# Moving a mixer's GpSimd arithmetic to VectorE, and keeping split weight operands in DRAM between two token halves

## The chip, the cores and the metric

The kernel runs on one core of a Trainium2 chip. The metric is the device time of one execution in microseconds (us). Five engines of the core work side by side, each on its own instruction stream: TensorE (PE in the profile; its weight loads are PEld), VectorE (DVE), ScalarE (ACT), GpSimd (POOL) and SyncE (SP), which here issues DMA transfers only. A measurement of this kernel tells apart differences of about 0.2%.

## The reference, cut to what matters

A two-layer decoder trunk over 1024 tokens of width 1024, in float32. Layer 0 mixes with a gated recurrence (HGRN2, four heads) and a retention (four heads); layer 1 mixes with an mLSTM (four heads). Each mixer and each MLP is wrapped in RMS norms.

```python
for l in range(DEPTH):
    g = norm_g[l]
    h = rmsnorm(x, g[0])
    y = even_mixer(h, ...) if l % 2 == 0 else odd_mixer(h, ...)
    x = x + rmsnorm(y, g[1])
    h = rmsnorm(x, g[2])
    x = x + rmsnorm(sq_relu_mlp(h, mlp_w1[l], mlp_w2[l]), g[3])
...
def even_mixer(h, w_in, ...):
    p = h @ w_in                       # 1024 x 5120
    hq, hf, hi, hgate, rq, rk, rv, rgate = jnp.split(p, splits, axis=-1)
    ...                                # scans over chunks, per-head norm, silu gates
    return y @ w_out
```

## The kernel before

**Stages.** The order is: even mixer on the first 512 tokens, even mixer on the second 512, first MLP on all tokens, odd mixer on the first half, odd mixer on the second, second MLP. Recurrent state goes from the first half to the second, so the halves are in order, and each half reads all weights of its mixer.

**Products.** A float32 product is made of three TensorE products of fp32r operands: every operand is split into `hi` (a rounded copy, made by ACT) and `lo` (the rest, a subtraction on DVE), and hi·hi, hi·lo and lo·hi are accumulated. On top of that a 2 x 2 block product is made of seven block products instead of eight (`combine`), which needs sums and differences of the weight blocks before they are split: four elementwise operations per set of four blocks, in `operands`. In the mixers a job is a *pair* (`p...`, `proj_pair`: seven operands of 128x512) or a *group* (`g...`, `proj_group`: seven operands of 128x1024, 24 matmuls of 256 columns for each). An even half has eight pairs and six groups, an odd half four and four, each followed by an output projection (`proj_tok`) whose 12 or 8 weight tiles are split without sums.

**The weight pipeline.** `raws` lists the weight tiles in the order of use; `pump` loads them on SP's queue into a ring of four buffers (`raw`, 512 KB each), and frees one when its last reader is done. `plan` lists the units; `next_units` has units prepared two ahead of the one it gives out. A unit is a pair of buffers `whi`, `wlo`, three of each. `split_w` (L157 to L161) makes hi on ACT and lo on DVE. The sums of `operands` (the helper is at L185 to L190) run on GpSimd in the mixers (`eng=nc.gpsimd`, rows of L190) and on DVE in the MLPs (L188). One buffer `ws` holds the sum of a21 and a22.

**Order.** The order within each engine's stream is made at build time by a scheduler that takes the ready instruction that stands first in the program. `tc.high_priority(offset=-100)` in `split_w`, in the MLP's `operands` and in `rest_operands` makes instructions count as if they stood 100 instructions later.

**Other GpSimd work.** In `right_sums` (L409) two of four differences of activation blocks, in `post_finish` (L496) the residual sum of the first half's output, in `silu_gate` (L609) the product of gate and sigmoid, in `rope` (L724) the last sum. The small [128 x 1] steps of the norms (`rsq`, L127 and L128) are on GpSimd too, and so are the DMA issues of the MLP's hidden activations (L1148).

**Chains.** Beside its products the even mixer has a chain for each HGRN head (`hg_chain`, L620): seven levels, each with four small score matmuls, a predicated copy (L664) and three products on DVE (L676 to L678) that the next level reads. Scans over four chunks follow (`hg_scan`, `rt_scan`, `ml_scan`).

Of the kernel before, what the change touches and what calls it, by code (L numbers as in the profile page):

```python
# [7 lines left out]
F32 = mybir.dt.float32  # L8
F32R = mybir.dt.float32r
# [6 lines left out]
P = 128  # L16
# [53 lines left out]
def hybrid_kernel(ctx, tc, x, norm_g, pv_d, cs_d, mk_d, dec_d, cos_d, sin_d, wg_d, gb_d, w_ev, w_od, w_mlp, out):  # L70
# [59 lines left out]

    raws = []
    MLP_UNITS = [0, 2, 4, *range(60), 60, 63, 61, 62, 60, 63, 61, 62]
    raws += [w_ev[u] for u in [*range(UE)] * 2]
    raws += [w_mlp[u] for u in MLP_UNITS]
    raws += [w_od[u] for u in [*range(UO)] * 2]
    raws += [w_mlp[64 + u] for u in MLP_UNITS]
    NRAW = 4
    loaded, count = [], {"taken": 0, "freed": 0, "given": 0}
# [1 line left out]
    def pump():  # L140
        while len(loaded) < min(count["freed"] + NRAW, len(raws)):
            i = len(loaded)
            raw = wp.tile([P, 1024], F32, tag="raw", bufs=NRAW, name=f"raw{i}")
            nc.sync.dma_start(out=raw, in_=raws[i])
            loaded.append(raw)

    def take_raw():
# [8 lines left out]

    def split_w(dst, src):  # L157
        hi, lo = dst
        with tc.high_priority(offset=-100):
            nc.scalar.copy(out=hi, in_=src)  # L160
            nc.vector.tensor_tensor(out=lo, in0=src, in1=hi.bitcast(F32), op=ALU.subtract)  # L161

    def new_pair(i):
        return (wp.tile([P, 1024], F32R, tag="hi", name=f"whi{i}"),
# [6 lines left out]
        free_raw()  # L171
        return hl

    def operands(wide, eng):

        if wide:
            a11, a21, a22, a12 = (take_raw() for _ in range(4))
            t = wp.tile([P, 1024], F32, tag="ws", bufs=1, name="ws")
        else:
            r1, r2 = take_raw(), take_raw()  # L180
            a11, a12 = r1[:, 0:512], r1[:, 512:1024]
            a21, a22 = r2[:, 0:512], r2[:, 512:1024]
            t = wp.tile([P, 1024], F32, tag="ws", bufs=1, name="ws")[:, 0:512]

        def op(o, x0, x1, f):  # L185
            if eng is nc.vector:
                with tc.high_priority(offset=-100):
                    eng.tensor_tensor(out=o, in0=x0, in1=x1, op=f)  # L188
            else:
                eng.tensor_tensor(out=o, in0=x0, in1=x1, op=f)  # L190

        op(t, a21, a22, ALU.add)
        yield a11
        yield t
        op(a21, a11, a21, ALU.subtract)
        op(a11, t, a11, ALU.subtract)
        yield a11
        yield a12
        op(a12, a12, a11, ALU.subtract)
        if wide:  # L200
            free_raw()
        yield a21
        if wide:
            free_raw()
        yield a12
        yield a22
        free_raw(2)

    def rest_operands():

        r1, r2 = take_raw(), take_raw()
        a11, a12 = r1[:, 0:512], r1[:, 512:1024]
        a21, a22 = r2[:, 0:512], r2[:, 512:1024]
        t = wp.tile([P, 1024], F32, tag="ws", bufs=1, name="ws")[:, 0:512]

        def op(o, x0, x1, f):
            with tc.high_priority(offset=-100):
                nc.vector.tensor_tensor(out=o, in0=x0, in1=x1, op=f)

        op(t, a21, a22, ALU.add)  # L220
        op(a21, a11, a21, ALU.subtract)
        op(a11, t, a11, ALU.subtract)
        yield a11
        yield t
        yield a21
        op(a12, a12, a11, ALU.subtract)
        yield a12
        yield a22
        free_raw(2)

    def pair_preps(n, eng=nc.gpsimd, begun=0):
        gen = {}
        todo = [(p, o, o == 0, o == last) for p in range(n) for last in [4 if p < begun else 6] for o in range(last + 1)]

        def prep(j):
            def run(i):
                hl = new_pair(i)
                for e, (p, o, first, last) in enumerate(todo[2 * j:2 * j + 2]):
                    if first:
                        gen[p] = rest_operands() if p < begun else operands(False, eng)  # L240
                    c = slice(e * 512, (e + 1) * 512)
                    split_w((hl[0][:, c], hl[1][:, c]), next(gen[p]))
                    if last:
                        next(gen[p], None)
                return hl
            return run
        return [prep(j) for j in range((len(todo) + 1) // 2)]

    def group_preps(eng=nc.gpsimd):
        gen = []  # L250

        def prep(o):
            def run(i):
                hl = new_pair(i)
                if o == 0:
                    gen.append(operands(True, eng))
                split_w(hl, next(gen[0]))
                if o == 6:
                    next(gen[0], None)
                return hl  # L260
            return run
        return [prep(o) for o in range(7)]

    BEGUN = 3

    def mlp_plan():
        units = [std_prep] * BEGUN + pair_preps(16, nc.vector, BEGUN)
        for _ in range(7):
            units += group_preps(nc.vector)
        return units + [std_prep] * 8  # L270

    plan = []
    for _ in range(2):
        for job in EV_JOBS:
            plan += group_preps() if job[0] == "g" else pair_preps(1)
        plan += [std_prep] * 12
    plan += mlp_plan()
    for _ in range(2):
        for job in OD_JOBS:
            plan += group_preps() if job[0] == "g" else pair_preps(1)  # L280
        plan += [std_prep] * 8
    plan += mlp_plan()
    ready = []

    def take_first():
# [3 lines left out]
    def next_units(j):  # L289
        n = count["given"]  # L290
        count["given"] += j
        while len(ready) < min(n + 3, len(plan)):
            ready.append(plan[len(ready)](len(ready)))
        return ready[n:n + j]
# [113 lines left out]

    def right_sums(stage):  # L409
        b11, b12, t1, t2, b21, t3, b22, t4 = (z[:, c] for z in stage for c in (L, R))  # L410
        for o, x0, x1, eng in ((t1, b12, b11, nc.vector), (t2, b22, t1, nc.vector),
                               (t3, b22, b12, nc.gpsimd), (t4, b21, t2, nc.gpsimd)):
            eng.tensor_tensor(out=o, in0=x0, in1=x1, op=ALU.subtract)  # L413

    def right_split(stage, k, p11, tiles):
        def split(dst, src):
# [76 lines left out]
        junk = sm.tile([P, 512], BF16, tag="junk", bufs=1, name="junk")  # L493
        nc.scalar.activation(out=junk, in_=y, func=AF.Square, accum_out=ss[t][:, n:n + 1])

    def post_finish(s, half, t, parts, ss, grow, tags=("z0", "z1"), eng=nc.gpsimd):  # L496
        tot = sm.tile([P, 1], F32, tag="tot", name=f"tot{s}_{half}_{t}")
        nc.gpsimd.tensor_tensor(out=tot, in0=ss[t][:, 0:1], in1=ss[t][:, 1:2], op=ALU.add)
        rs = sm.tile([P, 1], F32, tag="rs", name=f"rs{s}_{half}_{t}")
        rsq(rs, tot, 1.0 / D)  # L500
        xt = rg.tile([P, D], F32, tag=tags[t % len(tags)], name=f"xr{s}_{half}_{t}")
        nc.sync.dma_start(out=xt, in_=x_src(s, half * NT + t))
        s2 = sm.tile([P, 2], F32, tag="s2", name=f"s2{s}_{half}_{t}")
        for n in range(2):
            c = slice(n * 512, (n + 1) * 512)
            tmp = rg.tile([P, 512], F32, tag="tmp", bufs=2, name="ptmp")
            nc.vector.scalar_tensor_tensor(out=tmp, in0=parts[n], scalar=rs, in1=grow[:, c],
                                           op0=ALU.mult, op1=ALU.mult)
            eng.tensor_tensor(out=xt[:, c], in0=xt[:, c], in1=tmp, op=ALU.add)
            if s < 3:  # L510
                junk = sm.tile([P, 512], BF16, tag="junk", bufs=1, name="junk")
                nc.scalar.activation(out=junk, in_=xt[:, c], func=AF.Square, accum_out=s2[:, n:n + 1])
        nc.sync.dma_start(out=x_dst(s, half * NT + t), in_=xt)
        if s < 3:
            r = cp.tile([P, 1], F32, tag=f"rstd{half}_{t}", name=f"r{s}_{half}_{t}")
            nc.gpsimd.tensor_tensor(out=r, in0=s2[:, 0:1], in1=s2[:, 1:2], op=ALU.add)
            rsq(r, r, 1.0 / D)
            rstd[half, t] = r
        return xt
# [19 lines left out]
    def mixer_last(s, yT):  # L539
# [11 lines left out]
        xn = []  # L551
        for t in range(NT):
            post_sq(p1[t], t, 1, ss)
            xt = post_finish(s, 1, t, [y0[t], p1[t]], ss, grow, XT, nc.vector)
            parts = [kt.tile([P, HALF], F32, tag="kt", name=f"xk{s}_{t}_{n}") for n in range(2)]
            for n in range(2):
                nc.scalar.activation(out=parts[n], in_=xt[:, n * 512:(n + 1) * 512], func=AF.Copy, scale=rstd[1, t])
# [51 lines left out]
    def silu_gate(c, nm):  # L609
        for j in range(2):  # L610
            tmp = rg.tile([P, 2, 256], F32, tag="tmp", bufs=2, name=nm + f"sg{j}")
            nc.scalar.activation(out=tmp, in_=c[j], func=AF.Sigmoid)
            nc.gpsimd.tensor_tensor(out=c[j], in0=c[j], in1=tmp, op=ALU.mult)

    def scan_states(home, nm):

# [107 lines left out]
    def rope(c, cos, sin):  # L724
# [1 line left out]
        nc.vector.tensor_tensor(out=tmp[64:128], in0=c[0:64], in1=sin[0:64], op=ALU.mult)  # L726
        nc.vector.tensor_tensor(out=tmp[0:64], in0=c[64:128], in1=sin[64:128], op=ALU.mult)
        nc.vector.tensor_tensor(out=c, in0=c, in1=cos, op=ALU.mult)
        nc.gpsimd.tensor_tensor(out=c, in0=c, in1=tmp, op=ALU.add)

    def rt_keys(half, h, hT, cos, sin):
        nm = f"rt{half}_{h}"
# [691 lines left out]
```

## Time and profile before

| | |
|---|---|
| median of 3 runs | 2698.22 us (2695.55 to 2700.66) |
| the profiled execution | 2706.18 us, span 2704.4 us |
| busy: PE, PEld | 2467.0 us, 2239.8 us |
| busy: DVE, ACT, POOL | 1980.1 us, 1204.1 us, 780.4 us |
| moved by DMA | 335.91 MB, mean 124 GB/s |

Busy times are unions over the span; a matmul's end is modelled, so a busy PE may still be slower than it could be. The clock column (PEclk) is the share of full speed that the chip granted to TensorE.

### The profile page before, as it was taken

What the parts mean: (1) busy time and instruction counts of PE and PEld (TensorE: products, weight loads), DVE (VectorE), ACT (ScalarE), POOL (GpSimd) and SP (SyncE); (2) the same over time, 40 slices, a digit from 0 to 9 for tenths busy, and PEclk for the clock granted to TensorE, in tenths of its full rate; (3) what the DMA queues carried; (4) which work ended last, traced back from release to release, by engine and by line L of the source; (5) the groups of instructions that cost most, each with busy time, mean ns of one, the idle gap of its engine ahead of it and who ended that gap; (6) DMA issues with size and microseconds to landing.
All of it is one profiled execution on the core that took longest, in us unless ns stands there. A gap on an engine that the chain in (4) does not pass through costs nothing. (4 is left out here: it accounts for less than half of the span.)

```text
span 2704.4 us, 41553 instructions
## 1 busy us (share of the span) xinstructions
PE 2467.0 (91%) x16432; PEld 2239.8 (83%) x16432; DVE 1980.1 (73%) x2574; ACT 1204.1 (45%) x2080; POOL 780.4 (29%) x895
## 2 busy tenths in 40 slices
PE   6989998898897999999998688988988999999997
PEld 6888888898885888899997588888866888899996
DVE  7898868889748666657774798789757666766774
ACT  5444454444445443443344544554455434443332
POOL 5665437665311111100001345376320111100000
PEclk8999999999998999999999899999999999999999
DMA  3222323122232434453453222232233433554353
GB/s 137 69 73 78 110 86 118 63 79 71 94 140 102 168 144 156 171 198 126 160 172 125 103 87 79 100 133 69 96 134 108 169 145 140 210 178 136 129 174 140
DMA packets 92836, 335.91 MB, mean 124 GB/s; under 512 B 10848, under 2 KB 10976, under 8 KB 92640
## 3 DMA queue, kind: packets, MB, share of 16 engines
q1 hardware_dynamic: 75744, 272.42, 29.6%
q0 software_dynamic: 16896, 60.83, 5.9%
q8 instruction: 129, 2.11, 0.3%
q14 instruction: 67, 0.55, 0.1%
HBM read 255.61 MB, written 77.59 MB: 123 GB/s over the span
## 5 line engine op out<-in xcount | busy, mean ns | idle before, releaser
L160 ACT CAST whi<-raw 128x512 fp32r<-128x512 f32 (+1 forms) x590 | 469.6, 812 | 684.4 <-PE p_0x L1168 72.4
L161 DVE TENSOR_TENSOR wlo<-raw,whi 128x512 fp32r<-128x512 f32 (+1 forms) x590 | 583.7, 1005 | 192.3 <-ACT whi L160 174.1
L1279 POOL TENSOR_TENSOR rs<-pm 128x1 f32<-128x1 f32 (+1 forms) x7 | 2.2, 321 | 635.2 <-ACT junk L1263 635.2
L190 POOL TENSOR_TENSOR raw<-raw,raw 128x1024 f32<-128x1024 f32 (+1 forms) x64 | 151.1, 2361 | 83.3 <-DVE wlo L161 41.5
L160 ACT CAST whi<-ws 128x512 fp32r<-128x512 f32 (+1 forms) x90 | 70.4, 782 | 101.4 <-POOL ws L190 34.7
L190 POOL TENSOR_TENSOR raw<-ws,raw 128x512 f32<-128x512 f32 (+1 forms) x44 | 88.6, 2014 | 62.1 <-DVE wlo L161 42.1
L161 DVE TENSOR_TENSOR wlo<-ws,whi 128x512 fp32r<-128x512 f32 (+1 forms) x90 | 96.8, 1075 | 9.0 <-ACT whi L160 9.0
L190 POOL TENSOR_TENSOR ws<-raw,raw 128x1024 f32<-128x1024 f32 x20 | 51.1, 2555 | 39.3 <-DMA raw<-in_w_ev_dram 30.8
L322 DVE TENSOR_TENSOR ya<-p_0x,ya 128x1024 f32<-128x1024 f32 x26 | 31.8, 1222 | 34.9 <-PE p_0x L1169 34.9
L188 DVE TENSOR_TENSOR raw<-raw,raw 128x1024 f32<-128x1024 f32 (+1 forms) x54 | 52.0, 963 | 0.5
L413 POOL TENSOR_TENSOR xb_a<-xb_a,xb_a 128x256 f32<-128x256 f32 x32 | 34.2, 1079 | 56.4 <-ACT xb_a L479 50.4
L190 POOL TENSOR_TENSOR ws<-raw 128x512 f32<-128x512 f32 x24 | 36.3, 1513 | 46.8 <-DMA raw<-in_w_od_dram 25.5
L190 POOL TENSOR_TENSOR raw<-raw 128x512 f32<-128x512 f32 x24 | 36.7, 1528 | 32.4 <-DVE wlo L161 32.4
L1166 PE MATMUL p_0v<-whi,h_5R1h 128*128 128x256 f32 x128 | 36.6, 286 | 3.1 <-ACT h_5R1h L1019 3.1
L1166 PE MATMUL p_0v<-whi,h_1R0h 128*128 128x256 f32 x128 | 35.9, 281 | 2.9 <-ACT m_15h L340 2.9
L1168 PE MATMUL p_0v<-whi,h_5R1l 128*128 128x256 f32 x128 | 36.7, 287 | 1.8 <-DVE h_5R1l L1020 1.8
L1166 PE MATMUL p_0x<-whi,h_4L1h 128*128 128x256 f32 x128 | 35.8, 280 | 1.1 <-ACT whi L160 1.1
L1166 PE MATMUL p_0x<-whi,h_2L0h 128*128 128x256 f32 x128 | 36.0, 281 | 0.6 <-ACT ya L1173 0.6
L1169 PE MATMUL p_0v<-wlo,h_5R1h 128*128 128x256 f32 x128 | 36.4, 285 | 0.0
L1168 PE MATMUL p_0z<-whi,h_3L4l 128*128 128x256 f32 x128 | 35.9, 280 | 0.3 <-DVE h_3L4l L1020 0.3
L1168 PE MATMUL p_0v<-whi,h_1R0l 128*128 128x256 f32 x128 | 35.8, 280 | 0.0
L1169 PE MATMUL p_0x<-wlo,h_2L0h 128*128 128x256 f32 x128 | 35.8, 279 | 0.0
(5385 smaller groups left out, 10111.4 us busy)
## 6 DMA issues: line engine op xcount, KB each, us to landing
raw<-in_w_mlp_dram SPq DMA_DIRECT2D x142, 512.0 KB, 3.7
h<-hid SPq DMA_DIRECT2D x112, 512.0 KB, 4.3
raw<-in_w_ev_dram SPq DMA_DIRECT2D x104, 512.0 KB, 3.3
raw<-in_w_od_dram SPq DMA_DIRECT2D x64, 512.0 KB, 3.3
xs<-xr SPq DMA_DIRECT2D x24, 512.0 KB, 2.9
xr<-xs SPq DMA_DIRECT2D x24, 512.0 KB, 5.2
xn<-in_x_dram SPq DMA_DIRECT2D x8, 512.0 KB, 3.8
xr<-in_x_dram SPq DMA_DIRECT2D x8, 512.0 KB, 5.3
```

The costliest lines, as they stand in the source:

```text
L160: nc.scalar.copy(out=hi, in_=src)
L161: nc.vector.tensor_tensor(out=lo, in0=src, in1=hi.bitcast(F32), op=ALU.subtract)
L188: eng.tensor_tensor(out=o, in0=x0, in1=x1, op=f)
L190: eng.tensor_tensor(out=o, in0=x0, in1=x1, op=f)
L322: nc.vector.tensor_tensor(out=o, in0=x0, in1=x1, op=ALU.add)
L413: eng.tensor_tensor(out=o, in0=x0, in1=x1, op=ALU.subtract)
L1166: nc.tensor.matmul(a, h[:, c], hi[:, w], start=first and k == 0 and t % 2 == 0, stop=False, skip_group_check=True)
L1168: nc.tensor.matmul(a, l[:, c], hi[:, w], start=False, stop=False, skip_group_check=True)
L1169: nc.tensor.matmul(a, h[:, c], lo[:, w], start=False, stop=k == 3, skip_group_check=True)
L1279: nc.gpsimd.tensor_tensor(out=rs[:, z], in0=ss[half][:, 0, z], in1=ss[half][:, 1, z], op=ALU.add)
```

## The change

GpSimd's elementwise work of the mixers goes to DVE (sums of weight blocks, two differences in `right_sums`, the residual sum, the gate product, the last sum of `rope`). GpSimd keeps the [128 x 1] steps and the DMA issues of the hidden activations. In a mixer's first half each group's unit is also written to DRAM, hi and lo, right after its split. In the second half a group does no sums and no splits: units 0, 2 and 4 come through the ring of four raw buffers (two buffers for each, freed when the unit after next is asked for), units 1, 3, 5 and 6 are loaded into `whi` and `wlo`. Pairs and output projections are as before. All `high_priority(offset=-100)` are gone, in the MLPs too.

```diff
+    RING = (0, 2, 4)
+    kept = {}
+    def mixer_raws(w, jobs, n):
+        first, second, u = [], [], 0
+        for job in jobs:
+            m = 4 if job[0] == "g" else 2
+            mine = [w[u + i] for i in range(m)]
+            u += m
+            first += mine
+            if m == 4:
+                kept[n, job] = [[tc.dram_tile([P, 1024], F32, name=f"kw{n}_{job}_{o}{z}") for z in "hl"] for o in range(7)]
+                mine = [(F32R, z) for o in RING for z in kept[n, job][o]]
+            second += mine
+        last = [w[i] for i in range(u, n)]
+        return first + last + second + last
...
     def split_w(dst, src):
         hi, lo = dst
-        with tc.high_priority(offset=-100):
-            nc.scalar.copy(out=hi, in_=src)
-            nc.vector.tensor_tensor(out=lo, in0=src, in1=hi.bitcast(F32), op=ALU.subtract)
+        nc.scalar.copy(out=hi, in_=src)
+        nc.vector.tensor_tensor(out=lo, in0=src, in1=hi.bitcast(F32), op=ALU.subtract)
...
         def op(o, x0, x1, f):
-            if eng is nc.vector:
-                with tc.high_priority(offset=-100):
-                    eng.tensor_tensor(out=o, in0=x0, in1=x1, op=f)
-            else:
-                eng.tensor_tensor(out=o, in0=x0, in1=x1, op=f)
+            nc.vector.tensor_tensor(out=o, in0=x0, in1=x1, op=f)
...
-    def group_preps(eng=nc.gpsimd):
+    def group_preps(keep=None):
...
+                if keep:
+                    for d, z in zip(keep[o], hl):
+                        nc.sync.dma_start(out=d, in_=z.bitcast(F32))
                 return hl
...
+    held = {}
+    def kept_preps(keep):
+        def prep(o):
+            def run(i):
+                if o in RING:
+                    held[i] = 2
+                    return take_raw(), take_raw()
+                hl = new_pair(i)
+                for d, z in zip(keep[o], hl):
+                    nc.sync.dma_start(out=z.bitcast(F32), in_=d)
+                return hl
+            return run
+        return [prep(o) for o in range(7)]
+    def mixer_plan(jobs, n, outs):
+        units = []
+        for prep in (group_preps, kept_preps):
+            for job in jobs:
+                units += prep(kept[n, job]) if job[0] == "g" else pair_preps(1)
+            units += [std_prep] * outs
+        return units
...
     def next_units(j):
         n = count["given"]
         count["given"] += j
+        for i in [i for i in held if i < n]:
+            free_raw(held.pop(i))
...
-        for o, x0, x1, eng in ((t1, b12, b11, nc.vector), (t2, b22, t1, nc.vector),
-                               (t3, b22, b12, nc.gpsimd), (t4, b21, t2, nc.gpsimd)):
-            eng.tensor_tensor(out=o, in0=x0, in1=x1, op=ALU.subtract)
+        for o, x0, x1 in ((t1, b12, b11), (t2, b22, t1), (t3, b22, b12), (t4, b21, t2)):
+            nc.vector.tensor_tensor(out=o, in0=x0, in1=x1, op=ALU.subtract)
...
-            eng.tensor_tensor(out=xt[:, c], in0=xt[:, c], in1=tmp, op=ALU.add)
+            add(xt[:, c], xt[:, c], tmp)
...
-            nc.gpsimd.tensor_tensor(out=c[j], in0=c[j], in1=tmp, op=ALU.mult)
+            nc.vector.tensor_tensor(out=c[j], in0=c[j], in1=tmp, op=ALU.mult)
...
-        nc.gpsimd.tensor_tensor(out=c, in0=c, in1=tmp, op=ALU.add)
+        nc.vector.tensor_tensor(out=c, in0=c, in1=tmp, op=ALU.add)
```

## Rows read from the trace of the kernel before

**Rows 1.** The page's first part: the whole span, busy time of each engine.

```profile
span 2704.4 us, 41553 instructions
PE 2467.0 (91%) x16432; PEld 2239.8 (83%) x16432; DVE 1980.1 (73%) x2574; ACT 1204.1 (45%) x2080; POOL 780.4 (29%) x895
```

**Rows 2.** Busy time by stretch: even halves, MLP's two stages, odd halves.

```profile
core 0: us, PE busy (x) PEld busy (x) DVE busy (x) ACT busy (x) POOL busy (x), PEclk, DMA share, GB/s
28.00:335.00 307.00, 277.53 (x2196) 265.43 (x2197) 266.25 (x364) 136.10 (x265) 179.38 (x156) 0.95 0.25 83
...
424.00:730.00 306.00, 269.97 (x2147) 259.69 (x2146) 263.99 (x343) 136.21 (x266) 186.65 (x173) 0.96 0.25 83
...
842.00:1138.00 296.00, 293.41 (x1244) 235.62 (x1245) 198.44 (x305) 122.24 (x214) 41.20 (x60) 0.99 0.42 152
1138.00:1480.00 342.00, 324.97 (x2677) 320.80 (x2676) 230.27 (x208) 138.52 (x158) 10.25 (x12) 0.99 0.48 160
1480.00:1530.00 50.00, 28.01 (x194) 22.06 (x193) 36.70 (x49) 28.98 (x58) 20.97 (x18) 0.83 0.38 137
1530.00:1700.00 170.00, 151.24 (x1150) 145.88 (x1151) 148.54 (x223) 84.29 (x166) 76.86 (x86) 0.95 0.25 83
...
1767.00:1945.00 178.00, 154.86 (x1158) 148.73 (x1158) 154.86 (x223) 89.24 (x184) 105.30 (x110) 0.94 0.29 103
```

**Rows 3.** The same view, around single groups: two of the first half, one of the second.

```profile
80.50:111.30 30.80, 26.67 (x234) 25.49 (x234) 29.64 (x35) 12.24 (x20) 17.61 (x10) 1.00 0.20 69
287.50:320.80 33.30, 29.30 (x246) 28.28 (x246) 31.00 (x37) 12.52 (x21) 14.31 (x8) 0.95 0.30 103
471.30:505.20 33.90, 29.13 (x227) 28.65 (x226) 29.58 (x33) 13.43 (x26) 22.77 (x19) 0.90 0.19 63
```

**Rows 4.** PE's waits, 424:730 (who, released by: total us, times, longest), one row.

```profile
PE hg_1s L648 <- DVE hg_1ca L667: 4.3, 1, 4.3
```

**Rows 5.** By line and shape, 28:335, DVE, last ACT: count, busy us, mean ns, idle.

```profile
L161 DVE TENSOR_TENSOR wlo<-raw,whi 128x1024 fp32r<-128x1024 f32 x39 | 52.9, 1357 | 2.4 <-ACT whi L160 2.3
L677 DVE TENSOR_TENSOR hg_0qk<-hg_0qk,hg_0ts 128x256 f32<-128x256 f32 x7 | 8.4, 1195 | 0.0
L677 DVE TENSOR_TENSOR hg_3ca<-hg_3ca,hg_3ca 128x256 f32<-128x256 f32 x7 | 6.2, 886 | 0.0
L677 DVE TENSOR_TENSOR hg_2qk<-hg_2qk,hg_2ts 128x256 f32<-128x256 f32 x7 | 6.2, 885 | 0.0
...
L677 DVE TENSOR_TENSOR hg_1ca<-hg_1ca,hg_1ca 128x256 f32<-128x256 f32 x7 | 4.0, 574 | 0.0
...
L160 ACT CAST whi<-raw 128x1024 fp32r<-128x1024 f32 x39 | 40.8, 1048 | 43.4 <-POOL raw L190 9.8 <-PE rt_0px L307 5.7 <-PE rt_3px L307 5.1
```

**Rows 6.** Line L161 alone, and line L190 alone, busy in 28:335.

```profile
28.00:335.00 307.00, 102.98 (x96) 0.95 0.25 83
...
28.00:335.00 307.00, 106.24 (x52) 0.95 0.25 83
```

**Rows 7.** DVE by line and shape: 1138:1480 (first row), whole span (second).

```profile
L161 DVE TENSOR_TENSOR wlo<-raw,whi 128x1024 fp32r<-128x1024 f32 x49 | 59.7, 1218 | 14.1 <-ACT whi L160 14.1
...
L188 DVE TENSOR_TENSOR raw<-ws,raw 128x512 f32<-128x512 f32 x26 | 17.9, 689 | 0.5
```

**Rows 8.** POOL by line and shape, whole span.

```profile
L190 POOL TENSOR_TENSOR raw<-raw,raw 128x1024 f32<-128x1024 f32 x40 | 110.2, 2754 | 81.9 <-DVE wlo L161 41.5 <-issue 39.6
...
L413 POOL TENSOR_TENSOR xb_a<-xb_a,xb_a 128x256 f32<-128x256 f32 x32 | 34.2, 1079 | 56.4 <-ACT xb_a L479 50.4 <-DVE xb_a L413 4.8 <-DVE lbt L592 1.0
```

**Rows 9.** DMA: 1200:1260 in 40 slices (two rows); issues, 28:335; issues, page.

```profile
DMA  2878946566961808497118173718282789782000
GB/s 33 322 229 306 325 183 197 213 183 205 336 238 49 300 38 289 158 284 279 49 41 279 41 254 104 268 63 248 101 262 98 213 268 306 268 262 82 0 5 11
...
raw<-in_w_ev_dram SPq DMA_DIRECT2D x43, 512.0 KB, 3.3
...
xs<-xr SPq DMA_DIRECT2D x24, 512.0 KB, 2.9
```

More of the change, by code (lines that the diff above doesn't have):

```diff
@@ L132, in hybrid_kernel @@
     MLP_UNITS = [0, 2, 4, *range(60), 60, 63, 61, 62, 60, 63, 61, 62]
-    raws += [w_ev[u] for u in [*range(UE)] * 2]
+    RING = (0, 2, 4)
[13 more added lines that the diff above has]
+        return first + last + second + last
+    raws += mixer_raws(w_ev, EV_JOBS, UE)
     raws += [w_mlp[u] for u in MLP_UNITS]
-    raws += [w_od[u] for u in [*range(UO)] * 2]
+    raws += mixer_raws(w_od, OD_JOBS, UO)
     raws += [w_mlp[64 + u] for u in MLP_UNITS]
@@ L142, in pump @@
             i = len(loaded)
-            raw = wp.tile([P, 1024], F32, tag="raw", bufs=NRAW, name=f"raw{i}")
-            nc.sync.dma_start(out=raw, in_=raws[i])
+            dtype, src = raws[i] if isinstance(raws[i], tuple) else (F32, raws[i])
+            raw = wp.tile([P, 1024], dtype, tag="raw", bufs=NRAW, name=f"raw{i}")
+            nc.sync.dma_start(out=raw if dtype == F32 else raw.bitcast(F32), in_=src)
             loaded.append(raw)
@@ L172, in std_prep, with operands @@
         return hl
-    def operands(wide, eng):
+    def operands(wide):
         if wide:
@@ L216, in op @@
         def op(o, x0, x1, f):
-            with tc.high_priority(offset=-100):
-                nc.vector.tensor_tensor(out=o, in0=x0, in1=x1, op=f)
+            nc.vector.tensor_tensor(out=o, in0=x0, in1=x1, op=f)
         op(t, a21, a22, ALU.add)
@@ L229, in rest_operands, with pair_preps @@
         free_raw(2)
-    def pair_preps(n, eng=nc.gpsimd, begun=0):
+    def pair_preps(n, begun=0):
         gen = {}
@@ L239, in run @@
                     if first:
-                        gen[p] = rest_operands() if p < begun else operands(False, eng)
+                        gen[p] = rest_operands() if p < begun else operands(False)
                     c = slice(e * 512, (e + 1) * 512)
@@ L255, in run @@
                 if o == 0:
-                    gen.append(operands(True, eng))
+                    gen.append(operands(True))
                 split_w(hl, next(gen[0]))
@@ L262, in group_preps @@
         return [prep(o) for o in range(7)]
+    held = {}
[18 more added lines that the diff above has]
+        return units
     BEGUN = 3
     def mlp_plan():
-        units = [std_prep] * BEGUN + pair_preps(16, nc.vector, BEGUN)
+        units = [std_prep] * BEGUN + pair_preps(16, BEGUN)
         for _ in range(7):
-            units += group_preps(nc.vector)
+            units += group_preps()
         return units + [std_prep] * 8
[L272 to L282, printed above, removed]
+    plan = mixer_plan(EV_JOBS, UE, 12) + mlp_plan() + mixer_plan(OD_JOBS, UO, 8) + mlp_plan()
     ready = []
@@ L494, in post_sq, with post_finish @@
         nc.scalar.activation(out=junk, in_=y, func=AF.Square, accum_out=ss[t][:, n:n + 1])
-    def post_finish(s, half, t, parts, ss, grow, tags=("z0", "z1"), eng=nc.gpsimd):
+    def post_finish(s, half, t, parts, ss, grow, tags=("z0", "z1")):
         tot = sm.tile([P, 1], F32, tag="tot", name=f"tot{s}_{half}_{t}")
@@ L553, in mixer_last @@
             post_sq(p1[t], t, 1, ss)
-            xt = post_finish(s, 1, t, [y0[t], p1[t]], ss, grow, XT, nc.vector)
+            xt = post_finish(s, 1, t, [y0[t], p1[t]], ss, grow, XT)
             parts = [kt.tile([P, HALF], F32, tag="kt", name=f"xk{s}_{t}_{n}") for n in range(2)]
```

## The prediction

> **What bounds the kernel now.** I read the page's busy times first. PE is busy 91% of the span, DVE 73%, POOL 29% [rows 1]. An average of that kind says little here, so the next view was busy time by stretch [rows 2]. In the MLPs PE is nearly all there is: in 842:1138 it idles 2.6 us of 296, with DVE busy 198 (67%). In the mixers it is different. In the first even half (28:335) PE idles 29.5 us of 307 and in the second (424:730) 36; in the odd halves 19 of 170 and 23 of 178. DVE is busy 86 to 87% in all four, and the granted clock, which is the mean of the levels 2.4 and 1.2 GHz, is 0.94 to 0.96 there and 0.99 in the MLPs, where PE idles less. So what a mixer can give back is some 30 to 36 us of idle time per even half and about 12 us of lost clock (0.04 x 306), and 20 and 10 us per odd half.
>
> The third view says which engine makes PE wait. Around a single group DVE is busy 29.6 of 30.8 us, 31.0 of 33.3 and 29.6 of 33.9 [rows 3]. The products of a group are 7 x 24 matmuls; at the pace of the MLP's second stage, 325 us for 2677 [rows 2], that is 0.121 us each, 2.9 us a unit and 20.4 us a group. The stretches are 10 us longer; scans and small matmuls of other heads take part of this, and DVE, all but full, sets the rest. The list of PE's waits agrees: in the second even half they are short and scattered, a DVE step of an HGRN chain behind nearly all of them [rows 4].
>
> **Contention.** The same DVE instruction takes longer in the mixers. The 128x1024 subtraction of L161 takes 1.357 us in 28:335 [rows 5] and 1.218 in 1138:1480, where POOL is nearly idle [rows 7]. The four chain products of L677 have one shape and take between 0.574 and 1.195 us [rows 5]. And a sum on GpSimd takes 2.75 us at 128x1024 [rows 8], against 1.22 on DVE.
>
> How much DVE gets back without these sums, in an even half: at 1.22 and 0.69 us [rows 7] L161's 45 wide and 51 narrow subtractions would take 90 us in place of 103 [rows 6], 12.5% less. That share on all of DVE's 266 us is 33 us. The L677 rows would go from 24.8 us to 28 x 0.574 = 16.1, 35% less; that share on the 163 us that are not L161, and 13 on L161, is 70 us. I take 50, between the two, as DVE's other work mixes both kinds.
>
> The Trainium skill (SBUF — State Buffer, Who interferes with whom) says more: a DVE instruction with two SBUF inputs and a GpSimd instruction that reads SBUF lock one shared port, and the loser blocks for the whole instruction. By that, all of L190's 106 us in this half would be lost to DVE and come back; the sum would be twice my 50. The rows bear out less than half of it for the commonest instruction, so I stay with the rows.
>
> **The change part by part, in DVE time.** First even half: 24 wide and 28 narrow sums (the 52 of L190 [rows 6]) cost 24 x 1.22 + 28 x 0.69 = 48.6 us on DVE; 12 gate products and 8 rope sums at 0.69 cost 13.8. So DVE goes from 266 to 266 - 50 + 62 = 278 us (258 to 295 by the two bounds). That is 91% of the present stretch: as tight as now. In exchange each sum arrives 1.5 us sooner after its load. I take 0 for this half, from this alone between +15 and -15.
>
> Second even half: no sums and no splits for 6 groups, 42 x 1.22 = 51 us less, 28 pair sums (19) and gates and ropes (14) more: 264 - 50 - 51 + 33 = 196 us, 64% (176 to 213). That is the load of the MLP's first stage, where PE idles 1%. ACT loses 42 casts of 1.05 us [rows 5]. The upper bound of the gain is then all idle time and the lost clock, less 1%: 36 + 12 - 3 = 45 us; the lower one is 10, if DVE's relief ends only 2 us of waits in each of five groups. The chains' latency stays, so I take two thirds of 48, 32 us. Odd halves by the same steps: the first goes from 149 to 149 - 28 + 31 = 152 (0 gained), the second from 155 to 155 - 29 + 11 - 34 = 103 us; of 23 + 11 us two thirds are 22 (8 to 32).
>
> Where the next mixer starts (1480:1530, PE busy 28 of 50 [rows 2], and the same at the very start) `right_sums` stands on the path: two GpSimd differences of 1.08 us for each of four blocks [rows 8] become two of at most 0.6 on DVE. That is 1 us a block, 6 us over both places after something is lost to DVE's other work (2 to 10). The residual sums of `post_finish` lie beside an output projection and are costed at nothing; uncovered, 16 of them would give back 1 us each.
>
> DMA: 140 writes and 100 more reads (140 loads of kept tiles less 40 raw ones) of 0.524 MB, 126 MB on top of 336. In the first halves 84 and 56 writes lift 83 GB/s [rows 2] to 226 and 256 GB/s; in the second halves the loads give about 186 and 221. The busiest slices of the MLP show 322 and 336 GB/s at nine tenths busy or more [rows 9], so the rate has room on average, and in a second half units 1 and 3 can be loaded while a pair before the group is worked on. I cost the loads at nothing, covered by the products; without that cover a unit takes 1.05 MB / 336 GB/s = 3.1 us against 2.9, 0.2 us x 70 units = 14 us. For loads the Trainium skill (DMA: Bandwidth & Descriptors, Where 436 GB/s comes from) sets the limit for one core's HBM traffic at about 358 GB/s; by that a unit takes 2.93 us, and the cover would be exact. The SP queue gets 240 issues of 0.5 MB more, all in order. A write waits there for its `wlo`, and the raw loads behind it wait with it; as they already wait for the split that frees their buffer, I add nothing for this.
>
> The offset of -100 goes from every split. In the MLPs a split may then go ahead of an accumulator's eviction. DVE has 33% free there and PE does not wait, so I cost it at 0; the bounds are -5 and the rival below.
>
> Sum: 32 + 22 + 6 = 60 us less. The profiled execution took 2706.2 us, 1.8 more than its span, and lies 8.0 above the median of the three runs; 2706.2 - 60 = 2646, and by the same distance from the median, 2698.2 - 60 = **2638 us**.
>
> **Rivals.**
> *The writes hold the buffers* (slower). In a first half `whi` and `wlo` are free again only when their write has landed. Three pairs and 2.9 us a unit give 8.7 us for a cycle of cast (1.05), subtraction (1.22) and landing, so landing may take 6.4 us. Loads land in 3.3 us and writes in 2.9 when little else is queued [rows 9]; with three more transfers of 1.6 us in front of them (the sister write and two raw loads) it is 7.7, over the point. At 10 us a unit takes 1.2 us more, 84 us for 70 units, and the time is 2638 + 84 = 2722 us. For it: nothing today writes while a group is split. Against it: units are prepared two ahead, and a group now spreads over 31 to 33 us, not 20 [rows 3].
> *The chains, not DVE's load, hold PE* (about the same). Then the second halves gain only what contention costs the chain, say 5 us in all, with right_sums 6: 2687 us. For it: the waits listed are on chain steps [rows 4]. Against it: DVE's 93 to 96% around a group.
> *The split order costs PE in the MLPs* (about the same). 98 wide products, and half a split (0.6 us) lost at each, are 59 us, so 2697 us. Against it: PE's 1% idle and DVE's free third.
> *More comes back.* All idle time and clock in the second halves (45 + 32), 15 and 8 in the first ones, 10 at the starts: 110 us, so 2588 us.
>
> **How the numbers follow.** Chances: the forecast (2603 to 2673) 0.57, more 0.06, chains 0.11, split order 0.07, writes 0.19. What a measurement of this kernel can tell from no change is 0.2%, 5.4 us. Faster: forecast, more and most of the chains case, 0.71; within 0.2%: the rest of that case and half of the split order, 0.07; slower 0.22. The range reaches from the upper gain's edge to the writes' case: 2590 to 2725 us; the forecast's own, 2603 to 2673, is its sum with some 35 us to either side: the bounds of the terms come to 40 below and 55 above, and seldom all fall on one side.
>
> **What would show it.** Right: in the second halves DVE at 60 to 70%, groups of 25 us, the clock at 0.97 or more, and both stretches some 30 and 20 us shorter; L677 near 0.57 us for all heads; the first halves within 15 us of now. Wrong: PE or ACT in a first half waiting for a DMA landing on `kw`, writes landing later than 6.4 us, first halves of 330 us; PE waits on `wlo` or on an eviction in the MLPs; second halves no shorter with DVE at 64%.

## The result and the profile after

The changed kernel takes 2572.67 us (2571.97 to 2573.41, 4 runs) beside 2699.44 us of the kernel before (2695.55 to 2700.76, 4 runs): a ratio of 0.9533, 95% interval 0.9516 to 0.9549, or 127 us less. Its profiled execution has a span of 2571.6 us, 132.8 less than that of before (whose profiled execution lay 6.7 us above its median, so the stretches below add up to some 6 us more than the medians differ by). The forecast of 60 us had the sign right and less than half of the size, and the time lies below its range.

The first lines of the page after, which answer to [rows 1]:

```profile
span 2571.6 us, 41691 instructions
PE 2430.8 (95%) x16432; PEld 2213.6 (86%) x16432; DVE 1807.8 (70%) x2728; ACT 1138.0 (44%) x2010; POOL 303.2 (12%) x631
```

To say where the time went, both traces are cut at the same instructions: the first product of a half, the first matmul of its output projection, the first product of an MLP and of its second stage, the first transposition after it. Busy time by stretch, the kernel before; first even half, second, first MLP in its two stages, start of the odd mixer, its two halves:

```profile
core 0: us, PE busy (x) PEld busy (x) DVE busy (x) ACT busy (x) POOL busy (x), PEclk, DMA share, GB/s
22.30:333.10 310.80, 279.51 (x2199) 266.83 (x2199) 270.05 (x370) 139.26 (x272) 180.81 (x157) 0.94 0.24 82
...
412.70:723.40 310.70, 273.81 (x2200) 264.32 (x2198) 268.82 (x349) 138.02 (x274) 195.13 (x181) 0.96 0.26 89
...
802.50:1138.90 336.40, 318.57 (x1353) 254.89 (x1352) 230.69 (x346) 146.63 (x256) 50.06 (x76) 0.97 0.41 149
1138.90:1480.10 341.20, 324.17 (x2674) 320.15 (x2673) 229.37 (x207) 138.26 (x158) 9.68 (x11) 0.98 0.47 159
1480.10:1530.90 50.80, 28.44 (x198) 22.47 (x196) 36.70 (x49) 29.20 (x58) 20.97 (x18) 0.83 0.37 135
1530.90:1701.30 170.40, 152.01 (x1158) 146.67 (x1158) 149.14 (x223) 84.59 (x166) 76.86 (x86) 0.95 0.25 85
...
1766.90:1945.60 178.70, 154.99 (x1161) 148.85 (x1160) 155.46 (x223) 89.84 (x185) 105.40 (x110) 0.94 0.29 103
```

The same stretches after the change:

```profile
20.00:312.10 292.10, 275.13 (x2199) 264.09 (x2198) 257.24 (x447) 138.25 (x269) 36.44 (x76) 0.98 0.64 237
...
392.20:651.40 259.20, 257.39 (x2200) 251.74 (x2198) 180.55 (x362) 96.94 (x232) 39.58 (x100) 1.00 0.62 228
...
731.00:1067.40 336.40, 318.79 (x1353) 255.03 (x1352) 231.43 (x346) 146.69 (x256) 49.95 (x76) 0.97 0.42 149
1067.40:1408.00 340.60, 326.56 (x2676) 322.22 (x2675) 228.62 (x209) 138.73 (x158) 5.61 (x9) 0.98 0.48 159
1408.00:1446.00 38.00, 26.95 (x197) 21.74 (x195) 34.17 (x61) 26.53 (x56) 2.88 (x6) 0.91 0.40 149
1446.00:1600.20 154.20, 144.89 (x1156) 140.03 (x1155) 138.57 (x248) 87.24 (x169) 40.22 (x61) 1.00 0.76 280
...
1665.10:1812.40 147.30, 142.06 (x1160) 139.66 (x1159) 102.42 (x212) 64.24 (x158) 25.07 (x75) 1.00 0.72 264
```

Of the 132.8 us, 51.5 come from the second even half and 31.4 from the second odd one, 18.7 and 16.2 from the first halves, 12.8 from the start of the odd mixer and 2.3 from the start of the kernel. The MLPs take what they took. In the second halves PE idles 1.8 us of 259 and 5.2 of 147, and the granted clock is at the full 2.4 GHz; DVE is at 70% in both. In the first halves DVE is still at 88 and 90%, with more instructions in less time (447 in 257 us, 370 in 270 before).

DVE by line and shape in the first even half after the change; L179 and L707 are the lines L161 and L677 of before [rows 5]:

```profile
L179 DVE TENSOR_TENSOR wlo<-raw,whi 128x1024 fp32r<-128x1024 f32 x39 | 47.3, 1223 | 5.9 <-ACT whi L178 4.2 <-DMA kw_gh_2l<-wlo 0.7 <-ACT rv_3sg L642 0.6
...
L707 DVE TENSOR_TENSOR hg_0qk<-hg_0qk,hg_0ts 128x256 f32<-128x256 f32 x7 | 3.0, 433 | 0.0
L707 DVE TENSOR_TENSOR hg_1ca<-hg_1ca,hg_1ca 128x256 f32<-128x256 f32 x7 | 3.0, 426 | 0.0
```

The wide subtraction takes what it takes in the MLP [rows 7]. The chain product takes 0.43 us for both heads, less than the fastest head showed before, 0.574.

### The profile page after: what moved, and what is told of

It is laid out like the page before. It is cut to its first block, busy times and chain, and to the rows that moved or that the text cites. A ratio compares the mean times of both kernels' runs of the same rounds, so it can differ in the third digit from the quotient of the medians.

```text
span 2571.6 us, 41691 instructions
## 1 busy us (share of the span) xinstructions
PE 2430.8 (95%) x16432; PEld 2213.6 (86%) x16432; DVE 1807.8 (70%) x2728; ACT 1138.0 (44%) x2010; POOL 303.2 (12%) x631
## 3 DMA queue, kind: packets, MB, share of 16 engines
q8 instruction: 129, 2.11, 0.3%
## 5 line engine op out<-in xcount | busy, mean ns | idle before, releaser
L178 ACT CAST whi<-raw 128x512 fp32r<-128x512 f32 (+1 forms) x530 | 405.2, 786 | 635.6 <-PE p_0x L1198 68.6
L179 DVE TENSOR_TENSOR wlo<-raw,whi 128x512 fp32r<-128x512 f32 (+1 forms) x530 | 465.9, 895 | 195.9 <-ACT whi L178 179.9
L204 DVE TENSOR_TENSOR raw<-raw,raw 128x512 f32<-128x512 f32 (+1 forms) x98 | 93.0, 949 | 0.7
L179 DVE TENSOR_TENSOR wlo<-ws,whi 128x512 fp32r<-128x512 f32 (+1 forms) x80 | 67.7, 846 | 0.6 <-ACT whi L178 0.5
L204 DVE TENSOR_TENSOR raw<-ws,raw 128x512 f32<-128x512 f32 (+1 forms) x74 | 63.8, 862 | 0.9
L204 DVE TENSOR_TENSOR ws<-raw 128x512 f32<-128x512 f32 x50 | 34.5, 689 | 17.9 <-DMA raw<-in_w_mlp_dram 17.9
L204 DVE TENSOR_TENSOR ws<-raw,raw 128x1024 f32<-128x1024 f32 x24 | 29.4, 1224 | 18.3 <-DMA raw<-in_w_mlp_dram 16.8
L1199 PE MATMUL p_0v<-wlo,h_5R1h 128*128 128x256 f32 x128 | 36.4, 285 | 0.0
L1196 PE MATMUL p_0x<-whi,h_0L3h 128*128 128x256 f32 x128 | 36.0, 281 | 0.2
L1199 PE MATMUL p_0x<-wlo,h_0L3h 128*128 128x256 f32 x128 | 35.8, 280 | 0.0
L1199 PE MATMUL p_0x<-wlo,h_6L2h 128*128 128x256 f32 x128 | 35.8, 280 | 0.0
L1199 PE MATMUL p_0v<-wlo,h_1R0h 128*128 128x256 f32 x128 | 35.8, 279 | 0.0
```

The lines of the kernel that those rows point to most:

```text
L1196: nc.tensor.matmul(a, h[:, c], hi[:, w], start=first and k == 0 and t % 2 == 0, stop=False, skip_group_check=True)
L1199: nc.tensor.matmul(a, h[:, c], lo[:, w], start=False, stop=k == 3, skip_group_check=True)
```

## The experiments

Theory A: GpSimd's elementwise work stretches VectorE's instructions, and VectorE's time is what holds PE in a mixer; moving the work ends the stretch, and the copies in DRAM take more load off in the second halves. Rivals: the gain is only the work saved in the second halves (B), the order of the splits (D), or GpSimd's sums coming late, so that the splits which wait for them are late, rather than slowing VectorE's other instructions (E). All ratios are to the kernel before on the same chip. Stretches are cut as above.

**One part without the other.** `e1_vector_only` has no copies:

```diff
-                kept[n, job] = [[tc.dram_tile([P, 1024], F32, ...) for z in "hl"] for o in range(7)]
-                mine = [(F32R, z) for o in RING for z in kept[n, job][o]]
+                kept[n, job] = None
...
-        for prep in (group_preps, kept_preps):
+        for prep in (group_preps, group_preps):
```

> The changed kernel without the copies in DRAM: all elementwise mixer work on VectorE, the second half makes its sums and splits again, no offsets. Theory A (GpSimd's sums cost VectorE time by contention, and VectorE's load is what holds PE in a mixer): the first halves are as short as after the change, -20 and -16 us, the starts -13, and the second halves, now with the same VectorE load as the first ones, shorten by as much as these, -20 and -15; in all some -85 us, about 2615. Rival B (the gain is the saved work of the second halves, contention is minor): -35 at most for first halves and starts, second halves unchanged or longer, about 2665 or more.

Measured: 2604.92 us, ratio 0.9621 (0.9587 to 0.9654), 102 us less. Its four halves (even, odd):

```profile
19.50:307.50 288.00, 270.25 (x2198) 259.91 (x2198) 257.37 (x447) 137.60 (x269) 35.80 (x76) 0.96 0.26 87
387.60:675.20 287.60, 267.59 (x2198) 258.67 (x2197) 251.98 (x427) 137.82 (x275) 48.61 (x99) 0.98 0.29 96
...
1465.20:1620.00 154.80, 145.66 (x1159) 141.42 (x1159) 139.59 (x248) 87.27 (x169) 40.06 (x62) 0.99 0.31 101
1684.30:1847.30 163.00, 149.83 (x1161) 145.06 (x1159) 146.27 (x256) 90.22 (x185) 40.70 (x75) 0.97 0.31 106
```

Each even half is 23 us shorter, each odd one 16, somewhat more than expected, with no work saved anywhere. B falls. `e2_keep_only` is the other part: the kernel before, its offsets and GpSimd work included, with the copies.

```diff
+    raws += mixer_raws(w_ev, EV_JOBS, UE)
...
+                units += prep(kept[n, job], nc.gpsimd) if job[0] == "g" else pair_preps(1, eng=nc.gpsimd)
```

> The kernel before with the copies in DRAM alone: GpSimd keeps all its elementwise work (pair sums, gates, ropes, and the group sums of the first half), offsets as before. Theory A: the second halves gain nearly all that they gained by the whole change, as VectorE loses 42 and 28 splits there and GpSimd its group sums, -45 and -28 us; the first halves stay or lose a little to the writes, starts 0: about 2620 to 2630. Rival B: -85 in the second halves, about 2615. Rival C (contention alone matters, also from the pair sums, gates and ropes that stay): second halves only -25 and -15, about 2660.

Measured: 2630.9 us, ratio 0.9723 (0.9695 to 0.9750), 76 us less. Its two even halves:

```profile
21.70:337.60 315.90, 280.27 (x2197) 269.03 (x2198) 274.42 (x370) 139.73 (x272) 179.23 (x157) 0.93 0.59 219
417.30:680.60 263.30, 257.66 (x2195) 251.56 (x2193) 174.79 (x305) 96.70 (x233) 114.94 (x149) 1.00 0.61 223
```

The second even half alone gains 47 us, 4 less than with the whole change, with GpSimd still 115 us busy: once DVE has slack, being stretched costs little. The prediction's rival that the chains hold PE there, and not DVE's load, had put the second halves at 5 us together, and falls with it: the chain products still take 0.57 to 0.73 us as the mean of a head (0.42 to 0.43 in the changed kernel), and PE idles 5.6 us of 263. The two parts overlap: 100 and 73 us by their spans, 133 together, because a second half that PE fills cannot gain twice.

**The order.** `e3_offset_back` puts the blocks of -100 back into the changed kernel, `e4_offset_gone` takes them off the kernel before.

```diff
+        with tc.high_priority(offset=-100):
+            nc.scalar.copy(out=hi, in_=src)
+            nc.vector.tensor_tensor(out=lo, in0=src, in1=hi.bitcast(F32), op=ALU.subtract)
...
+            with tc.high_priority(offset=-100):
+                nc.vector.tensor_tensor(out=o, in0=x0, in1=x1, op=f)
```

> The changed kernel with the offsets of -100 back on every split and on the weight sums on VectorE. Theory A: within 0.3% of the changed kernel, 2565 to 2581 us. Rival D (part of the unexpected gain comes from the order of the splits): at least 15 us slower, 2588 or more.

> The kernel before with the offsets of -100 taken off, nothing else. Theory A: within 0.3% of the kernel before, 2691 to 2707 us. Rival D: 2684 or less, and the first halves shorter.

Measured: 2575.06 us, ratio 0.9516 (0.9486 to 0.9546), and 2703.06 us, ratio 0.9991 (0.9976 to 1.0007). Both as theory A has it; D falls. The program that is built from the kernel before is the same with 0 in place of -100, so, other than the section on the kernel before says, that number sets nothing back by 100 instructions here; taking the block off does change the order.

**Contention or lateness.** `e5_idle_sums` gives GpSimd sums that nobody reads:

```diff
+    def beside(wide, on):
+        if on:
+            for _ in range(2 if wide else 1):
+                nc.gpsimd.tensor_tensor(out=idle, in0=idle, in1=idle, op=ALU.add)
...
         def op(o, x0, x1, f):
+            beside(wide, on)
             nc.vector.tensor_tensor(out=o, in0=x0, in1=x1, op=f)
```

> The changed kernel with GpSimd sums that nobody needs: beside each weight sum that VectorE makes in a mixer, GpSimd adds a 512-wide scratch to itself (twice beside a 1024-wide sum), so as much as it did before the change, in the first halves. Theory A (contention): VectorE's instructions of the first even half stretch again, busy 257 us to over 290 for the same work, and the first halves lose what the move gave them or more, +20 and +15 us; the second halves, with free VectorE time, lose under 5 each; total +35 to +50, some 2615. Rival E (GpSimd's sums cost by coming late, not by contention): nobody waits for these sums, so within 5 us of the changed kernel.

Measured: 2680.83 us, ratio 0.9914 (0.9886 to 0.9941), by the spans 108 us more than the changed kernel, 88 of them in the first even half and 20 before it. The size was not as expected, for a reason that the tile's own rows show: the sums wait for nothing, so all 176, those of the odd mixer too, ran in the first 366 us.

```profile
L198 POOL TENSOR_TENSOR idle<-idle x176: 1033/1367/2112, 1.5 to 364.5; 128x512 f32<-128x512 f32 x176
```

That makes the first even half the test and the odd halves the control:

```profile
40.20:420.70 380.50, 300.73 (x2198) 283.24 (x2198) 352.28 (x442) 136.90 (x267) 242.49 (x231) 0.91 0.49 181
...
1551.20:1706.00 154.80, 145.12 (x1155) 140.40 (x1154) 137.97 (x246) 87.09 (x169) 40.52 (x61) 1.00 0.75 280
1770.90:1918.20 147.30, 142.09 (x1161) 139.46 (x1160) 103.16 (x212) 64.75 (x158) 24.92 (x75) 1.00 0.71 263
```

In the first even half the same DVE work takes 352 us in place of 257, 95 us for 206 us of added GpSimd time, 0.46 us for each, and the half is 88 us longer. Where no idle sum ran, nothing changed. Since nobody reads the sums, lateness is no part of it: contention is shown. It is not shown that lateness cost nothing in the kernel before; more on this under `e8_rest_moved`.

Single instructions of the kernel before show how the contention works. Two products of L677 beside sums of GpSimd, each pair in order of start (start, duration):

```profile
79.89 2.43 POOL L190 TENSOR_TENSOR raw<-raw,raw 128x1024 f32<-128x1024 f32 x1
80.02 2.58 DVE L677 TENSOR_TENSOR hg_0qk<-hg_0qk,hg_0ts 128x256 f32<-128x256 f32 x1
...
180.39 0.41 DVE L677 TENSOR_TENSOR hg_1ca<-hg_1ca,hg_1ca 128x256 f32<-128x256 f32 x1
180.42 2.64 POOL L190 TENSOR_TENSOR ws<-raw,raw 128x1024 f32<-128x1024 f32 x1 [1.25 <-DMA raw<-in_w_ev_dram]
```

The product that started second ended 0.28 us after the sum; the one that started first took 0.41 us. The kernel before has 56 products of L677. In 19 a GpSimd addition or product of 0.9 us or more was running at their start; each of them ends 0.28 to 0.29 us after it and takes 1.48 to 2.63 us. The other 37 take 0.41 to 0.44 us. GpSimd waits too: 28 of the idle sums above start while no VectorE sum, difference or product runs and take 1.04 us in the median, the other 148 take 1.37 us and up to 2.11.

**The writes.** `e6_no_writes` writes one unit per mixer and has every load read that one:

```diff
-                if keep:
+                if keep and o == 0 and keep is first_kept(keep):
                     for d, z in zip(keep[o], hl):
...
```

> The changed kernel with 2 writes per mixer instead of 84 and 56: only the first group's first unit goes to DRAM, and all loads of the second half read it (so the second half's weights are not the reference's, its traffic is). Theory A: the first even half gains 4 us, the odd one nothing, as the kernel without copies showed; 2565 to 2575. The prediction's rival (the writes hold the buffers): the first halves gain 10 us or more each, 2550 or less.

Measured: 2568.53 us, ratio 0.9497 (0.9472 to 0.9522). Its first halves:

```profile
20.20:307.40 287.20, 269.49 (x2198) 258.73 (x2198) 257.05 (x447) 137.79 (x269) 35.72 (x76) 0.97 0.28 91
...
1437.30:1591.80 154.50, 146.56 (x1161) 142.01 (x1160) 139.55 (x248) 86.97 (x169) 39.96 (x62) 0.99 0.32 105
```

Without the writes the first even half takes 287.2 us here and 288.0 in the kernel without copies; with them it takes 292.1, 295.7 (`e3_offset_back`) and 294.5 (`e11_after_again`). So 84 writes cost it some 5 us, which the runs' times do not part from noise, and 56 writes cost the odd one nothing. `e9_writes_gpsimd` issues them from GpSimd's queue, so that raw loads don't stand behind them (`nc.sync` to `nc.gpsimd` at the write).

> The changed kernel with the first half's writes issued by GpSimd instead of SyncE, so that raw loads no longer stand behind writes that wait for their split. If the 5 us that the writes cost in the first even half come from this order: 3 to 5 us faster than the changed kernel beside it, 287 to 289 us in that half. If they come from the bytes or from buffers held, no change. If GpSimd's small norm steps get stuck behind the writes: slower, scans late, 10 us or more.

Measured: 2580.59 us, ratio 0.9551 (0.9537 to 0.9566), with `e11_after_again`, the changed kernel once more, beside it at 2574.28 us, ratio 0.9530 (0.9516 to 0.9544). Its first halves:

```profile
20.10:317.10 297.00, 275.48 (x2198) 263.14 (x2198) 257.81 (x447) 136.89 (x269) 82.82 (x160) 0.95 0.62 233
...
1449.00:1608.50 159.50, 147.92 (x1159) 142.90 (x1158) 138.93 (x249) 89.06 (x171) 69.33 (x117) 0.98 0.75 279
```

The even one takes 297.0 us, against 292.1 and 294.5 in two profiles of the changed kernel, and the odd one, in which the writes cost nothing, 159.5 against 154.2 and 155.0. GpSimd is busy 46 and 29 us more. So issuing them there seems to have a price of its own, and the run does not tell whether SP's order is what the writes cost: their order, their bytes and the buffers all stay open.

> The changed kernel once more, beside the other two on the same chip: 0.951 to 0.955 of the kernel before.

**Which of GpSimd's work.** Without copies, `e7_sums_moved` moves only the weight sums to DVE, `e8_rest_moved` only the rest (`eng=nc.gpsimd` kept in `right_sums`, `post_finish`, `silu_gate`, `rope`, or in `operands`).

> No copies, and only the weight sums on VectorE; the two differences of right_sums, the residual sums, gate products and rope sums stay on GpSimd. Theory A: most of GpSimd's elementwise time is in the weight sums, so all four halves gain about three quarters of the kernel with everything on VectorE, -17 and -12 us each, and the start of the odd mixer stays at 51 us: about -60, 2645.

> No copies, and only the rest on VectorE: right_sums, residual sums, gate products and rope sums; the weight sums stay on GpSimd. Theory A: the start of the odd mixer is 12 us shorter, the halves gain 3 to 8 us each: about -30, 2675. If the parts do not add up to the -102 of the kernel with everything on VectorE, the remainder comes from the two together.

Measured: 2619.17 us, ratio 0.9686 (0.9663 to 0.9708), and 2675.24 us, ratio 0.9895 (0.9873 to 0.9918). The sums bring 84 us (60 were expected) and the rest 28, where both together brought 102. Their first even halves, the sums alone moved and the rest alone:

```profile
20.30:309.60 289.30, 271.38 (x2199) 260.35 (x2199) 259.61 (x424) 137.50 (x270) 74.20 (x101) 0.96 0.27 87
```

```profile
22.00:321.90 299.90, 274.02 (x2199) 263.71 (x2199) 271.35 (x395) 138.89 (x270) 144.41 (x132) 0.97 0.26 85
```

With the rest alone moved, the half is 10.9 us shorter than before although DVE is as busy (271.4 us for 270.1). So DVE's busy time is not all that counts. Results that come sooner (E) could do this, and so could steps of a chain that are no longer stretched while other work fills DVE; no run parts the two. The start of the odd mixer with the sums alone moved, and with the rest alone:

```profile
1430.40:1470.50 40.10, 27.34 (x196) 21.61 (x194) 33.75 (x53) 27.50 (x56) 10.16 (x14) 0.91 0.39 142
```

```profile
1458.30:1502.40 44.10, 28.67 (x216) 24.00 (x216) 37.05 (x57) 28.24 (x57) 12.52 (x10) 0.91 0.34 129
```

Here the expectation missed: 40.1 us with `right_sums` still on GpSimd, not 51. Either part alone takes GpSimd from 21 to 10 or 13 us busy; they give 10.7 and 6.7 of the 12.8 us (12 were expected of the rest alone).

**Does VectorE still hold the first halves?** `e10_no_group_sums` leaves the groups' weight sums out of the first halves:

```diff
         def op(o, x0, x1, f):
-            nc.vector.tensor_tensor(out=o, in0=x0, in1=x1, op=f)
+            if sums:
+                nc.vector.tensor_tensor(out=o, in0=x0, in1=x1, op=f)
...
-        yield t
+        yield t if sums else a22
```

> The changed kernel without the groups' weight sums in the first halves (so its weights are not the reference's): VectorE is relieved of 24 and 16 instructions of 1.22 us, 29 and 20 us, and nothing else is changed. If VectorE's load still sets the first halves: the even one goes from 292 to 270 or less, the odd one from 154 to 147 to 149; in all some -25 us, 2548. If what is left there is the latency of the chains and the writes: under 8 us less, 2565.

Measured: 2540.29 us, ratio 0.9406 (0.9391 to 0.9422).

```profile
20.20:291.80 271.60, 265.96 (x2199) 258.40 (x2198) 231.32 (x423) 136.94 (x269) 36.52 (x76) 0.99 0.68 255
...
1421.00:1566.90 145.90, 142.54 (x1160) 139.73 (x1159) 124.87 (x234) 85.80 (x168) 23.83 (x61) 1.00 0.79 298
```

26 us less DVE time make the even half 20.5 us shorter, 14 us the odd one 8. So DVE still holds these halves, at 0.8 and 0.6 us for each us of its work; part of this can be the step between a load and its split, which is left out with the sums. `e12_silu` takes work off DVE without leaving any out: ScalarE's Silu in place of a Sigmoid and a DVE product.

```diff
-            nc.scalar.activation(out=tmp, in_=c[j], func=AF.Sigmoid)
-            nc.vector.tensor_tensor(out=c[j], in0=c[j], in1=tmp, op=ALU.mult)
+            nc.scalar.activation(out=c[j], in_=c[j], func=AF.Silu)
```

> The changed kernel with ScalarE's Silu in place of Sigmoid and a product on VectorE, for the gates and the HGRN queries of the even mixer: 16 VectorE instructions of 0.69 us less in each half, 11 us. By the slope that the kernel without group sums showed (20.5 us shorter for 26 us less VectorE time, 0.8) the first even half gets 8 to 9 us shorter, about 284; the second, which PE fills, stays at 259; total -9, 2564. If ScalarE has to change its function table between Sigmoid, Silu and the rest, it gets busier and the gates come later: 0 to 10 us slower in both even halves.

Measured: 2571.29 us, ratio 0.9511 (0.9495 to 0.9527): against 0.9530 (0.9516 to 0.9544) the intervals overlap. In its profile, of an execution of 2560.67 us:

```profile
20.00:307.00 287.00, 269.51 (x2198) 258.72 (x2199) 248.75 (x431) 147.10 (x276) 33.16 (x77) 0.97 0.65 241
```

DVE has 248.8 us of work in the first even half in place of 257.2, the half is 287.0 us long, and ACT has 9 us more to do: 16 table loads of 1.28 us in both halves together that the changed kernel does not have. A gain of some us is likely, and not shown.

## Why the prediction was wrong, step by step

Of the 73 us between the forecast's 60 and the 132.8 by the spans, 35 lie in the first halves, 29 in the second ones and 9 at the starts. The mechanism, that DVE holds PE in the mixers and GpSimd slows DVE, was right; sizes were not.

**VectorE's relief was mis-sized, and that is the step that failed.** It was put at 50 us per even half, between 33 and 70. Measured by the prediction's own sums for the work that was added or saved: 270 + 62 - 257 = 75 in the first even half, 70 in the second (269 - 51 + 33 - 181), 41 and 30 in the odd ones for 28 and 29. The upper bound took the mean of the fastest head of L677, 0.574 us [rows 5], for an undisturbed product, but GpSimd had slowed one of that head's seven too; the others took 0.41 to 0.44. The lower bound came from L161, 1.357 against 1.218 us, which suffers little. The products of `rope`, which the sum did not read, suffer far more. That head's seven products (shortest, median, longest in ns), and a row of `rope` before and after:

```profile
L677 DVE TENSOR_TENSOR hg_1ca<-hg_1ca,hg_1ca x7: 409/414/1521, 151.1 to 180.4; 128x256 f32<-128x256 f32 x7
...
L726 DVE TENSOR_TENSOR rtmp<-rt_0kq,rot 64x512 f32<-64x512 f32 x2 | 4.0, 1978 | 0.1
...
L756 DVE TENSOR_TENSOR rtmp<-rt_0kq,rot 64x512 f32<-64x512 f32 x2 | 1.4, 684 | 0.1
```

The sixteen products of `rope` (L726, L727) went from 24 to 11 us in the first even half. The predicated copies (L664), which read their data from the matmuls' memory (PSUM), took 0.74 us before, after and beside the idle sums.

The rule of the Trainium skill on the shared port (SBUF — State Buffer, Who interferes with whom) was set aside because it seemed to give twice as much. Read as it stands, it makes the port an exclusive lock and has issue order decide who blocks; it does not say that all of a GpSimd sum is lost to VectorE. The trace of the kernel before agrees, as its L677 products show. So the prediction misread it when it had all of L190's 106 us lost. What a us of GpSimd costs VectorE depends on who starts first, and these runs give it: 75 us came back for the 144 us that GpSimd's busy time fell (180.8 to 36.4), 0.52 us for each, and the idle sums cost 0.46 us for each.

**The first halves at nothing** was wrong by 18.7 and 16.2 us. DVE was forecast at 278 us in the even one, 8 more than before, and came to 257, 13 less. A us of DVE time was worth 0.8 us in the kernel without group sums and 0.93 beside the idle sums, so these 13 us account for 10 to 12 of the 18.7. The rest is not DVE's busy time, as `e8_rest_moved` showed, and its cause stays open. The conclusion "as tight as now" read the busy share; the share did stay, 87 to 88%, while the stretch shrank with the work.

**The second halves** gave 51.5 and 31.4 us where 32 and 22 were forecast. The mechanism was right: DVE at 70% (64 forecast), PE full. Two thirds was too little, and in the even half the bound of 45 was too low: of the 51.5 us 35 were idle time of PE, and PE's busy time itself fell by 16.4, from 273.8 to 257.4 us, more than the 12 allowed for the clock; no row says where the other 4 come from. "The chains' latency stays" was wrong; PE's longest waits in the second even half, before ([rows 4] is the second of its list) and after:

```profile
PE hg_0s L648 <- ACT whi L160: 4.5, 1, 4.5
...
PE rt_3kt L770 <- DVE gate L818: 0.5, 1, 0.5
PE rt_2o L806 <- DVE s_rt L810: 0.5, 1, 0.5
PE rv_1y L348 <- DMA whi<-kw_gr_1h: 0.3, 1, 0.3
```

**The starts** gave 15.1 us for 6, in the odd mixer by more than the two differences, as the two partial moves showed.

**The rival "more comes back"**, 110 us at a chance of 0.06, came closest, and each of its terms was passed: 83 us for 77 in the second halves, 35 for 23 in the first, 15 for 10 at the starts.

**The loads at nothing** held: PE's only larger wait for one is 3.3 us in the second odd half, at 264 GB/s. **The offset at nothing** held, and the first MLP took 336.4 and 340.6 us for 336.4 and 341.2. Whether **the SP queue** cost nothing is not shown, as `e9_writes_gpsimd` did not tell. The Trainium skill's limit for HBM traffic (DMA: Bandwidth & Descriptors, Where 436 GB/s comes from), about 358 GB/s for one core, was not reached as a mean in any stretch, but it is no ceiling here: slices of 7.3 us of the first even half after the change moved up to 415 GB/s. That wait, and these slices:

```profile
PE mv_0y L348 <- DMA whi<-kw_g_1h: 3.3, 1, 3.3
...
GB/s 16 58 188 380 337 413 53 323 108 318 352 342 81 65 85 278 278 320 379 144 311 344 358 388 4 144 2 275 159 364 349 296 102 295 324 276 367 415 96 87
```

**The rival of the writes** came near: issues in the first even half, KB each, median us to landing, from early to late units of a group.

```profile
kw_gr_1l<-wlo SPq DMA_DIRECT2D x4, 512.0 KB, 2.6
...
kw_gr_4l<-wlo SPq DMA_DIRECT2D x4, 512.0 KB, 5.3
...
kw_gr_6l<-wlo SPq DMA_DIRECT2D x4, 512.0 KB, 8.4
```

Late units are over the 6.4 us from which it was to decide; but only at the end of a group, with a pair next, and the price was some 5 us, not 84.

## What to carry to other kernels

Where two engines slow each other, take an instruction's undisturbed time from its shortest instances, or from a stage in which the other engine is idle, not from the fastest mean of the disturbed stage; and price the relief for all the work of the stage. The trace of the kernel before held this number: six of the seven products behind the mean of 0.574 us took 0.41 to 0.44. An engine's busy share says that it is the bound, not that a change which keeps the share gains nothing: what counts is its work in us. An upper bound of a gain from PE's idle time and clock can be too low: PE's busy time fell by 4 us more than the clock's share here.

## What was not expected of the hardware

Additions on GpSimd whose operands nobody else touches made VectorE's work 95 us longer for 206 us of GpSimd time. A VectorE product of 0.41 us that starts while a GpSimd sum runs ends 0.28 us after that sum, up to 2.6 us later than it started; one that starts first is not slowed. DMA carried 280 GB/s as the mean of 154 us in the first odd half, writes and reads mixed, at no cost that these runs can show. And a weight-sized write that is issued by GpSimd instead of SyncE made the first even half no shorter, 297.0 us, and the first odd one 159.5 us for 154.2 and 155.0.
